# A hybrid decoder layer on one Trainium2 core: the last block's top-k queued behind the gate build, four U chunks held for its end, the late pools split in two, index transposes queued behind U chunks

## The chip, the cores and the metric

The kernel runs on one core of a Trainium2 chip, as one program without loops at run time: the Python loops below are unrolled into one instruction stream for each engine. The engines are PE (matmuls), DVE (VectorE), ACT (ScalarE), POOL (GpSimd) and SP, which only issues DMAs here. The metric is the device time of one execution in microseconds; a comparison takes the median of several.

## The reference, cut to what matters

One decoder layer for 512 tokens of width 1024: a normalised, modulated input goes through latent attention and retention, an output projection and a residual; then comes PEER, a layer of 16384 one-neuron experts, and a last RMSNorm. The change lies in PEER:

```python
q = (xt @ w_query).reshape(T, 8, 2, 128)
s = jnp.einsum('thpd,pkd->thpk', q, sub_keys)          # 8 heads x 2 halves x 128 keys
s_top, i_top = lax.top_k(s, 16)
cand = s_top[:, :, 0, :, None] + s_top[:, :, 1, None, :]
best, pos = lax.top_k(cand.reshape(T, 8, 256), 16)      # 128 experts a token
eidx = ...                                              # i*128 + j of the chosen pairs
g = softmax(best)
a = gelu(einsum('thkd,td->thk', expert_u[eidx], x))
out = einsum('thk,thkd->td', g * a, expert_v[eidx])
```

## The kernel before, in words

The 512 tokens are four blocks of 128. PEER is computed in two ways. Blocks 0 to 2 (`DB`) go the dense way: all 16384 experts are applied to all 384 tokens, with a gate that is zero where an expert was not chosen. Block 3 (`GB`) goes the sparse way: POOL gathers the chosen rows of `expert_u` and `expert_v` by indirect DMA, 128 of each, and DVE multiplies and sums them.

Products in float32 are made of three matmuls (`mm3`) on a rounded part and its remainder: for every streamed weight chunk ACT makes `hi` and DVE or POOL makes `lo` (`split`, L70).

**Top-k** (`topk`, L606). For each block DVE finds the 16 best of 128 for 8 heads and 2 halves, then the 16 best of 50 candidate sums, and turns positions into indices with one-hot comparisons in float16 tiles `t4k`. A softmax follows (one Exp on ACT). For dense blocks the indices and gates are transposed on PE (L673 to L675, under `tc.high_priority()`) into `it` and `gt`. For block 3 they become the index list `eidx` (L667) and `gsm`. The tiles of the pool `topk` are single-buffered, so blocks share them: the index tile `i1` and the tile `iF` that the transposes read are one buffer.

**U chunks** (`u_chunk`, L736). One of 128 chunks of 128 experts: a 512 KB load (`raw`, three buffers), hi and lo, 24 matmuls of 384 columns into a PSUM bank `ab` (two), and a Gelu into `ga` or `gb`. There are 26 `ga` and 11 `gb` buffers: chunk c with c mod 37 below 26 goes into `ga`, others into `gb`; chunk 37 needs chunk 0's.

**Gate build** (`g_steps`, L759). For 8 tokens a step, 48 steps in all: DVE writes four one-hot tiles (L770 to L773, `ohs`, three buffers), PE multiplies them, ACT copies the products into `stg` (two buffers of 2 MB), and after every fourth step SP stores `stg` to DRAM (`Gd`, L786), 12 stores.

**V chunks** (`v_load`, `v_mm`). For 128 experts: `vraw` is loaded, hi and lo made (lo on POOL while U chunks are left), the gate tile `gtl` (L796) is read back from `Gd` once in four chunks, DVE multiplies it with `ga` into `wf` (L807), ACT and DVE split that into `wh` and `wl`, and 18 matmuls add into six PSUM banks.

**Order of the work.** The program is traced in the order of the code. Tile's scheduler then orders each engine's instructions by a simulated time line and by their place in the trace, so an instruction that is traced late can be placed early where its engine would idle. The engines execute in that fixed order and wait at semaphores. Inside `tc.manual_schedule` an engine keeps the traced order. In the code: the top-k of blocks 0 to 2 (L751); 36 U chunks (`R0`) with two gate steps in front of each of the first 24 (L849); the top-k of block 3 (L856); then one pool `late` for everything that follows, which lies where the top-k and gate-build tiles were, with `reuse_waits="tile"`, so that a new tile waits for the old ones under it; then 124 rounds of V chunk c and U chunk c + 36 (L898). Each round adds 2.5 (later 1.12) to a credit, and each whole unit issues one gather step. POOL has manual order from L897, so its vlo and gathers run as traced. The last four V chunks and the final norm close the kernel.

Of the kernel before, what the change touches and what calls it, by code (L numbers as in the profile page):

```python
# [8 lines left out]
F32 = mybir.dt.float32  # L9
# [6 lines left out]
OP = mybir.AluOpType  # L16
# [12 lines left out]
ND = len(DB)  # L29
GB = 3  # L30
# [3 lines left out]
R0 = 36  # L34
RA = 26
NC_ = 50
GPU = 2
GSC = float(2 ** 14)
HB = 2
LB = 4  # L40
CR = (2.5, 1.12)
ORDER = "L m0! p1 d3 p2! m1 p3 d4 p4 d2 p5 p6 r0! r1! p7 r2 r3 X0 X1! d5! m2 g! m3 w0 X3 X2 h0 w1 q0 q1! h1 q2 q3"


# [1 line left out]
def build(ctx: ExitStack, tc: tile.TileContext, A, out):  # L46
    nc = tc.nc
    V, S, P, T, G = nc.vector, nc.scalar, nc.gpsimd, nc.tensor, nc.sync
# [28 lines left out]
    def mm3(o, wh, wl, rh, rl, start, stop, skip=False):  # L77
        T.matmul(o, wh, rh, start=start, stop=False, skip_group_check=skip)  # L78
        T.matmul(o, wh, rl, start=False, stop=False, skip_group_check=skip)  # L79
        T.matmul(o, wl, rh, start=False, stop=stop, skip_group_check=skip)  # L80

    pf = ctx.enter_context(ExitStack())
    ptk = ctx.enter_context(ExitStack())
# [21 lines left out]
    for hf in range(2):  # L105
        p = tpb()
# [49 lines left out]
    hh = cp.tile([128, NB, 8, 128], R, name="hh")  # L156
    hl = cp.tile([128, NB, 8, 128], R, name="hl")
# [445 lines left out]
            w //= 2  # L603
        e.tensor_add(dst, t[:, 0], t[:, 1])

    def topk(b):  # L606
        v1 = tk.tile([128, 8, 2, 16], F32, name="v1", bufs=1)
        i1 = tk.tile([128, 8, 2, 16], U32, name="i1", bufs=1)
        for h in range(8):
# [53 lines left out]
        if b == GB:  # L663
# [2 lines left out]
                                   ij[:, 1].rearrange("p k h -> p (k h)"), op0=OP.mult, op1=OP.add)  # L666
            V.tensor_copy(eidx, ef)  # L667
            return
        with tc.high_priority():
            iF = tk.tile([128, 2, 128], F32, name="i1", bufs=1)  # L670
            V.tensor_copy(iF, ij.rearrange("p q k h -> p q (k h)"))
            p = ob()
            T.transpose(p[:, :128], iF[:, 0], ident)  # L673
            T.transpose(p[:, 128:256], iF[:, 1], ident)
            T.transpose(p[:, 256:384], gg, ident)  # L675
            it = tk.tile([128, 2, 128, 2], F16, name=f"it{b}")
            gt = tk.tile([128, 2, 128, 2], F16, name=f"gt{b}")
            two = lambda a, n: a[:, :, None].to_broadcast([128, n, 2])
            S.activation(it.rearrange("p q t w -> p (q t) w"), two(p[:, :256], 256), AF.Copy)
            S.activation(gt[:, 0], two(p[:, 256:384], 128), AF.Copy, scale=GSC)  # L680
            V.scalar_tensor_tensor(gt[:, 1], two(p[:, 256:384], 128), GSC, gt[:, 0], op0=OP.mult, op1=OP.subtract)
# [51 lines left out]
    NT = ND * 128  # L733
    gas = {}

    def u_chunk(c, lo_engine):  # L736
        raw = raw_t()
        G.dma_start(raw, A["uT"][c])
        hi, lo = split(raw, lo_engine)
        p = ab()  # L740
        for k in range(8):
            ks = slice(k * 128, (k + 1) * 128)
            mm3(p[:, :NT], hi[:, ks], lo[:, ks], hh[:, :ND, k, :], hl[:, :ND, k, :], k == 0, k == 7)
        if c % (R0 + 1) < RA:
            ga = dn.tile([128, NT], F32, name="ga", bufs=RA)
        else:
            ga = dn2.tile([128, NT], F32, name="gb", bufs=R0 + 1 - RA)
        S.activation(ga, p[:, :NT], AF.Gelu)  # L748
        gas[c] = ga

    for b in DB:  # L751
        topk(b)
    pf.close()

    Gd = dram.tile([NIG, ND * 128 // TGS, 128, IGN, TGS], F32, name="Gd")
# [3 lines left out]
    def g_steps():  # L759
        for d, b in enumerate(DB):  # L760
            ij, gg = idxT[b], gT[b]
            for tg in range(128 // TGS):
                stg = gp.tile([128, 128, TGS], F32, name="stg", bufs=2)
                for t8 in range(TGS // 8):
                    t0 = tg * TGS + t8 * 8
                    ohs = gp.tile([128, 4, 8, 128], F16, name="ohs", bufs=3)
                    oh = [ohs[:, q].rearrange("p t (a w) -> p t a w", w=2) for q in range(4)]
                    io = iota_h.rearrange("p (a w) -> p a w", w=2)[:, None].to_broadcast([128, 8, 64, 2])
                    bc = lambda a: a[:, t0:t0 + 8, None, :].to_broadcast([128, 8, 64, 2])
                    V.tensor_tensor(oh[0], io, bc(ij[:, 1]), op=OP.is_equal)  # L770
                    V.tensor_tensor(oh[1], io, bc(ij[:, 0]), op=OP.is_equal)
                    V.tensor_tensor(oh[2], oh[1], bc(gg[:, 0]), op=OP.mult)
                    V.tensor_tensor(oh[3], oh[1], bc(gg[:, 1]), op=OP.mult)  # L773
                    for t4 in range(2):
                        p = tpb() if t4 else acc()
                        for t in range(4):
                            u = t4 * 4 + t
                            cs = slice(t * 128, (t + 1) * 128)
                            T.matmul(p[:, cs], ohs[:, 0, u], ohs[:, 2, u], start=True, stop=False)
                            T.matmul(p[:, cs], ohs[:, 0, u], ohs[:, 3, u], start=False, stop=True)  # L780
                        o0 = t8 * 8 + t4 * 4
                        S.activation(stg[:, :, o0:o0 + 4], p.rearrange("p (t i) -> p i t", t=4), AF.Copy,
                                     scale=1.0 / GSC)
                    yield
                ti = d * (128 // TGS) + tg
                G.dma_start(Gd[:, ti].rearrange("g j i t -> j g (i t)"),  # L786
                            stg.rearrange("p (g i) t -> p g (i t)", i=IGN))
# [32 lines left out]
    gacc = []  # L820

    def gather(table, s):
        r = lp.tile([128, 1024], F32, name="grow", bufs=4)
        P.indirect_dma_start(out=r, out_offset=None, in_=A[table],  # L824
                             in_offset=bass.IndirectOffsetOnAxis(ap=eidx[:, s:s + 1], axis=0))
        return r

    def gather_steps():
        for s in range(128):
            r = gather("expert_u", s)  # L830
            jk = st.tile([128, 1024], BF, name="junk", bufs=1)
            V.scalar_tensor_tensor(jk, r, 1.0, h2n, op0=OP.mult, op1=OP.mult, accum_out=asl[:, s:s + 1])  # L832
            yield
        S.activation(wsl, asl, AF.Gelu)
        V.tensor_mul(wsl, wsl, gsm)
        for i in range(2):
            g = lp.tile([128, 1024], F32, name=f"gacc{i}")
            gacc.append(g)
        for s in range(128):
            r = gather("expert_v", s)  # L840
            g = gacc[s % 2]
            if s < 2:
                V.tensor_scalar(g, r, wsl[:, s:s + 1], None, op0=OP.mult)
            else:
                V.scalar_tensor_tensor(g, r, wsl[:, s:s + 1], g, op0=OP.mult, op1=OP.add)  # L845
            yield

    gs = g_steps()
    for c in range(R0):  # L849
        for _ in range(GPU):  # L850
            next(gs, None)
        u_chunk(c, P if c < 8 else V)
    for _ in gs:
        pass
    pg_.close()
    topk(GB)  # L856
    ptk.close()
    lp = ctx.enter_context(tc.tile_pool(name="late", bufs=1, side="right", reuse_waits="tile"))
    gt2 = lp.tile([128, 1024], F32, name="gt2")
    row_bc(5, gt2)  # L860
    h2n = lp.tile([128, 1024], F32, name="h2n")
    G.dma_start(h2n, h2d)
    gfb = lp.tile([128, 1024], F32, name="gfb")
    G.dma_start(gfb, A["g_final"].partition_broadcast(128))
    asl = lp.tile([128, 128], F32, name="asl")
    wsl = lp.tile([128, 128], F32, name="wsl")
    vacc += [acc() for _ in range(3)] + [tpb() for _ in range(2)] + [ob()]
    ga_it = gather_steps()

    h01 = (slice(0, 512), slice(512, 1024))  # L870

    def final_x(b):
        x2 = raw_t()
        G.dma_start(x2, x2d[b])
        t = lp.tile([128, 1024], F32, name="grow", bufs=4)
        ss = lp.tile([128, 2], F32, name="ssf", bufs=2)
        return x2, t, ss

    def final_h(f, hf, p, eng):
# [5 lines left out]

    def final_b(b, f):
        x2, t, ss = f
        rr = lp.tile([128, 1], F32, name="rrf", bufs=2)
        V.tensor_add(rr, ss[:, 0:1], ss[:, 1:2])
        V.tensor_scalar(rr, rr, 1.0 / D, EPS, op0=OP.mult, op1=OP.add)  # L890
        P.tensor_tensor(rr, rr, mhalf[:, :1], op=OP.pow)
        for cs in h01:
            V.scalar_tensor_tensor(t[:, cs], x2[:, cs], rr, gfb[:, cs], op0=OP.mult, op1=OP.mult)
            G.dma_start(out[b * 128:(b + 1) * 128, cs], t[:, cs])

    credit = 0.0
    ctx.enter_context(tc.manual_schedule(engines={mybir.EngineType.Pool}))  # L897
    for c in range(NK - LB):  # L898
        w = v_load(c)
        for d in range(ND):  # L900
            v_mm(c, w, d)
        if c + R0 < NK:
            u_chunk(c + R0, V)
        credit += CR[0] if c + R0 < NK else CR[1]
        while credit >= 1:
            credit -= 1
            next(ga_it, None)
# [87 lines left out]
```

## Time and profile before

| | us |
|---|---|
| median of 3 runs (1637.5 to 1643.1) | 1642.41 |
| the profiled execution | 1639.2 |
| its span | 1637.3 |
| busy PE / DVE / POOL / ACT | 1522.5 / 1303.1 / 893.8 / 622.7 |

The span runs from the first to the last instruction. The engines' busy shares of the whole span (93%, 80%, 55%, 38%) mix stages with different limits, so the stages are read apart: the front of the layer up to about 440 us, top-k and gate build with U chunks up to about 690, the loop of U and V chunks up to about 1470, V chunks alone and the final norm to the end. "PEclk" is the granted TensorE clock in parts of full speed.

### The profile page before, as it was taken

The page shows a single profiled execution, that of the slowest core. Times are in us where ns is not written, and L with a number is a line of the kernel's source. Part 1 is how long each engine was busy: PE and PEld are TensorE (multiplying, and loading weights), DVE is VectorE, ACT ScalarE, POOL GpSimd, SP SyncE. Part 2 cuts the span into 40 slices and gives each one's busy share as a digit, 9 for nine tenths or more (in the row PEclk, how much of TensorE's full clock was granted, in tenths as well). Part 3 has the DMA queues.
Part 4 walks back from the last instruction along what each step waited for, and adds up shares of the span by engine and source line. Part 5 has one row for each costly group of instructions (what it writes and reads, how often), then busy time and mean ns, then how long its engine had stood idle before and what let it go on. Part 6 is the DMA issues. An engine that isn't in the chain of part 4 may idle for free.

```text
span 1637.3 us, 24259 instructions
## 1 busy us (share of the span) xinstructions
PE 1522.5 (93%) x8977; PEld 1375.7 (84%) x8977; DVE 1303.1 (80%) x2315; ACT 622.7 (38%) x1009; POOL 893.8 (55%) x521
## 2 busy tenths in 40 slices
PE   6899999997878999769999999999999999999977
PEld 6889987797878998667999999999999999988866
DVE  7975754639999999959888787788877887798874
ACT  4433244444424554433333333333333333333322
POOL 4532742775530000058777777777676767775544
PEclk9999999999999999779999999999999999999999
DMA  9455440554325667699989888889988898989853
GB/s 359 156 197 168 143 144 29 183 162 142 104 77 175 211 204 223 208 302 321 337 306 315 286 317 312 296 304 310 333 310 295 301 334 295 321 304 308 284 186 103
DMA packets 196041, 395.63 MB, mean 242 GB/s; under 512 B 12241, under 2 KB 111569, under 8 KB 195922
## 3 DMA queue, kind: packets, MB, share of 16 engines
q1 hardware_dynamic: 157906, 257.22, 46.4%
q0 software_dynamic: 36864, 134.23, 23.5%
q10 hardware_dynamic: 1152, 2.62, 0.4%
q8 instruction: 70, 1.15, 0.3%
q14 instruction: 49, 0.40, 0.1%
HBM read 364.15 MB, written 29.88 MB: 241 GB/s over the span
## 4 chain that ended last, share of the span: by engine, by line
PE 65%; DVE 21%; DMA 5%; issue 4%; POOL 4%; ACT 1%; SPq 0%; DVEq 0%; POOLq 0%; ACTq 0%
PE ab L80 8%; PE ab L78 8%; PE ab L79 8%; PE acc L80 7%; PE acc L78 7%; PE acc L79 7%; PE tp L78 3%; PE tp L79 3%; PE tp L80 3%; DVE lo L74 2%; PE ob L80 1%; PE ob L79 1%; PE ob L78 1%; DVE gacc L845 1%; DVE ohs L770 1%
## 5 line engine op out<-in xcount | busy, mean ns | idle before, releaser
L74 POOL TENSOR_TENSOR vlo<-vraw,vhi 128x1024 fp32r<-128x1024 f32 x92 | 235.7, 2561 | 345.7 <-ACT vhi L73 345.1
L78 PE MATMUL ab<-hh,hi 128*128 128x384 f32 x1024 | 347.1, 339 | 21.7 <-ACT ga L748 19.5
L73 ACT ACTIVATE hi<-raw 128x1024 fp32r<-128x1024 f32 x204 | 216.1, 1060 | 391.4 <-PE ab L79 264.7
L80 PE MATMUL ab<-hh,lo 128*128 128x384 f32 x1024 | 347.7, 340 | 3.8 <-DVE lo L74 2.7
L79 PE MATMUL ab<-hl,hi 128*128 128x384 f32 x1024 | 346.3, 338 | 0.0
L74 POOL TENSOR_TENSOR lo<-raw,hi 128x1024 fp32r<-128x1024 f32 x71 | 181.3, 2556 | 178.6 <-ACT hi L73 170.7
L832 DVE SCALAR_TENSOR_TENSOR junk<-grow,h2n 128x1024 bf16<-128x1024 f32 x128 | 208.6, 1629 | 65.3 <-DMA grow<-in_expert_u_dram,eidx 64.2
L845 DVE SCALAR_TENSOR_TENSOR gacc<-grow,wsl,gacc 128x1024 f32<-128x1024 f32 x126 | 206.4, 1649 | 57.8 <-DMA grow<-in_expert_v_dram,eidx 55.9
L78 PEld LDWEIGHTS ab<-hh,hi 128*128 128x128 f32 x1024 | 193.7, 189 | 26.8 <-ACT ga L748 20.6
L824 POOL DMA_INDIRECT grow<-in_expert_u_dram,eidx x128 | 183.2, 1431 | 39.9 <-issue 22.7
L80 PEld LDWEIGHTS ab<-hh,lo 128*128 128x128 f32 x1024 | 193.6, 189 | 5.7 <-DVE lo L74 4.1
L79 PEld LDWEIGHTS ab<-hl,hi 128*128 128x128 f32 x1024 | 193.7, 189 | 3.4
L824 POOL DMA_INDIRECT grow<-in_expert_v_dram,eidx x128 | 173.5, 1355 | 37.8 <-issue 23.0
L74 DVE TENSOR_TENSOR lo<-raw,hi 128x1024 fp32r<-128x1024 f32 x133 | 171.7, 1291 | 22.9 <-ACT hi L73 16.6
L809 ACT ACTIVATE wh<-wf 128x384 fp32r<-128x384 f32 x110 | 57.8, 525 | 276.4 <-issue 229.2
L79 PE MATMUL acc<-vlo,wh 128*128 128x512 f32 x330 | 129.3, 392 | 9.5 <-DVE vlo L74 5.8
L73 ACT ACTIVATE vhi<-vraw 128x1024 fp32r<-128x1024 f32 x110 | 115.2, 1049 | 39.2 <-DMA vraw<-in_expert_v_dram 39.2
L80 PE MATMUL acc<-vhi,wl 128*128 128x512 f32 x330 | 130.0, 394 | 0.0
L78 PE MATMUL acc<-vhi,wh 128*128 128x512 f32 x330 | 128.8, 397 | 0.0
L78 PE MATMUL acc<-hi,hh 128*128 128x256 f32 (+2 forms) x296 | 91.6, 317 | 6.3 <-ACT hi L73 3.8
L810 DVE TENSOR_TENSOR wl<-wf,wh 128x384 fp32r<-128x384 f32 x110 | 85.5, 777 | 14.6 <-ACT wh L809 14.5
L79 PE MATMUL acc<-lo,hh 128*128 128x256 f32 (+2 forms) x296 | 93.4, 316 | 1.5 <-DVE lo L74 0.8
(339 smaller groups left out, 3332.2 us busy)
## 6 DMA issues: line engine op xcount, KB each, us to landing
raw<-in_uT_dram SPq DMA_DIRECT2D x128, 512.0 KB
vraw<-in_expert_v_dram SPq DMA_DIRECT2D x110, 512.0 KB
Gd<-stg SPq DMA_DIRECT2D x12, 2048.0 KB
gtl<-Gd SPq DMA_DIRECT2D x32, 768.0 KB
raw<-in_wadaT_dram SPq DMA_DIRECT2D x40, 512.0 KB
raw<-in_w_query_dram SPq DMA_DIRECT2D x32, 512.0 KB
raw<-in_expert_v_dram SPq DMA_DIRECT2D x18, 512.0 KB
raw<-in_w_out_dram SPq DMA_DIRECT2D x16, 512.0 KB
```

Of the source, the lines that this page charges most:

```text
L73: S.activation(hi[:, :n], raw[:, :n], AF.Copy)
L74: lo_engine.tensor_sub(lo[:, :n], raw[:, :n], hi[:, :n].bitcast(F32))
L78: T.matmul(o, wh, rh, start=start, stop=False, skip_group_check=skip)
L79: T.matmul(o, wh, rl, start=False, stop=False, skip_group_check=skip)
L80: T.matmul(o, wl, rh, start=False, stop=stop, skip_group_check=skip)
L770: V.tensor_tensor(oh[0], io, bc(ij[:, 1]), op=OP.is_equal)
L809: S.activation(wh, wf, AF.Copy)
L810: V.tensor_sub(wl, wf, wh.bitcast(F32))
L824: P.indirect_dma_start(out=r, out_offset=None, in_=A[table], in_offset=bass.IndirectOffsetOnAxis(ap=eidx[:, s:s + 1], axis=0))
L832: V.scalar_tensor_tensor(jk, r, 1.0, h2n, op0=OP.mult, op1=OP.mult, accum_out=asl[:, s:s + 1])
L845: V.scalar_tensor_tensor(g, r, wsl[:, s:s + 1], g, op0=OP.mult, op1=OP.add)
```

## The change

The second number in `UF` is the count of U chunks that are traced ahead of the top-k of that block. `tc.issue_after(ins)` places each instruction that its block traces on ins's engine behind `ins` in that engine's order; it adds no semaphore. So the index transposes of blocks 1 and 2 stand behind U chunk 7 and 15 on PE, the held chunks' matmuls behind the last gate matmul and their lo behind the last one-hot, and all DVE instructions of block 3's top-k behind the last one-hot. The gate build gets three steps a chunk over chunks 16 to 31, one step being left for the end. Block 3's top-k is traced after two rounds of the V loop. The pool `late` becomes `vside` (V tiles, opened after the gate build) and `gside` (gather and final tiles, opened after block 3's top-k); manual order of POOL begins there.

```diff
+HOLD = 4
+UF = {1: 8, 2: 16}
+LEAD = 2
-CR = (2.5, 1.12)
+CR = (2.56, 1.12)
...
-        with tc.high_priority():
+        with tc.issue_after(after) if after else tc.high_priority():
             iF = tk.tile([128, 2, 128], F32, name="i1", bufs=1)
...
+    def u_load(c):
+        raw = raw_t()
+        G.dma_start(raw, A["uT"][c])
+        return raw
+    def u_chunk(c, lo_engine, raw=None):
+        raw = u_load(c) if raw is None else raw
...
+        last["u"] = m.ins
...
+    nu = 0
     for b in DB:
-        topk(b)
+        while nu < UF.get(b, 0):
+            u_chunk(nu, P if nu < 8 else V)
+            nu += 1
+        topk(b, last.get("u"))
...
     gs = g_steps()
-    for c in range(R0):
-        for _ in range(GPU):
-            next(gs, None)
+    left = ND * 16
+    for c in range(nu, R0 - HOLD):
+        n = -(-left // (R0 - HOLD - c))
+        for _ in range(min(n, left - 1)):
+            next(gs)
+            left -= 1
         u_chunk(c, P if c < 8 else V)
+    held = [u_load(c) for c in range(R0 - HOLD, R0 - HOLD + 3)]
     for _ in gs:
         pass
+    with tc.issue_after(last["g"]):
+        with tc.issue_after(last["o"]):
+            for i, c in enumerate(range(R0 - HOLD, R0)):
+                u_chunk(c, V, held[i] if i < 3 else None)
     pg_.close()
-    topk(GB)
-    ptk.close()
-    lp = ctx.enter_context(tc.tile_pool(name="late", bufs=1, side="right", reuse_waits="tile"))
+    lp = ctx.enter_context(tc.tile_pool(name="vside", bufs=1, reuse_waits="tile"))
...
     for c in range(NK - LB):
+        if c == LEAD:
+            with tc.issue_after(last["o"]):
+                topk(GB)
+            ptk.close()
+            lg = ctx.enter_context(tc.tile_pool(name="gside", bufs=1, side="right", reuse_waits="tile"))
+            h2n = lg.tile([128, 1024], F32, name="h2n")
+            G.dma_start(h2n, h2d)
...
+            ga_it = gather_steps(h2n, asl, wsl)
+            ctx.enter_context(tc.manual_schedule(engines={mybir.EngineType.Pool}))
         w = v_load(c)
         for d in range(ND):
             v_mm(c, w, d)
         if c + R0 < NK:
             u_chunk(c + R0, V)
+        if c < LEAD:
+            continue
         credit += CR[0] if c + R0 < NK else CR[1]
```

`last["o"]` is the last one-hot (L773), `last["g"]` the last gate matmul (L780).

## Rows read from the trace of the kernel before

**Rows 1.** Busy time by stretch: length, engines with (xinstructions), PE clock, DMA share, GB/s
```profile
464.30:694.30 230.00, 208.86 (x1642) 196.44 (x1641) 226.75 (x661) 107.36 (x177) 7.21 (x3) 0.95 0.60 187
...
800.00:1400.00 600.00, 600.00 (x3048) 546.90 (x3047) 485.07 (x497) 212.79 (x291) 438.48 (x254) 1.00 0.88 310
...
688.00:700.00 12.00, 3.26 (x22) 2.52 (x20) 5.91 (x14) 2.28 (x4) 0.00 (x0) 0.50 0.66 193
700.00:712.00 12.00, 3.25 (x10) 3.25 (x11) 3.26 (x6) 4.98 (x7) 1.49 (x1) 0.50 0.92 299
...
609.00:610.00 1.00, 1.00 (x7) 1.00 (x6) 1.00 (x9) 0.00 (x0) 0.00 (x0) 1.00 0.95 291
```

**Rows 2.** Waits of PE and DVE, 400 to 720 us: total, times, longest
```profile
PE ab L78 <- ACT ga L748: 19.5, 3, 16.8
PE ob L673 <- DVE i L671: 18.2, 2, 9.7
...
DVE wf L807 <- DMA gtl<-Gd: 11.5, 1, 11.5
```

**Rows 3.** Single lines: count, duration, first and last start (L748, L74, L786)
```profile
L748 ACT ACTIVATE ga<-ab x32: 466/472/512, 447.0 to 763.5; 128x384 f32<-128x384 f32 x32
L748 ACT ACTIVATE gb<-ab x11: 471/472/493, 606.3 to 664.5; 128x384 f32<-128x384 f32 x11
...
L74 DVE TENSOR_TENSOR lo<-raw,hi x33: 1200/1221/1240, 492.5 to 679.0; 128x1024 fp32r<-128x1024 f32 x33
...
L786 SPq DMA_DIRECT2D Gd<-stg x12: 377/377/383, 503.9 to 690.8; - x12
```

**Rows 4.** DVE in order of time: start, duration, instruction, [idle before, releaser]
```profile
393.81 3.23 DVE L643 TENSOR_TENSOR t4k<-t4k,dd 128x2048 f16<-128x2048 f16 x1
...
463.21 0.29 DVE L671 CAST i<-ij 128x256 f32<-128x256 f16 x1
...
659.36 0.70 DVE L771 TENSOR_TENSOR ohs<-iota_h,it 128x1024 f16<-128x1024 f16 x1
659.96 0.70 DVE L772 TENSOR_TENSOR ohs<-ohs,gt 128x1024 f16<-128x1024 f16 x1
...
661.89 1.23 DVE L74 TENSOR_TENSOR lo<-raw,hi 128x1024 fp32r<-128x1024 f32 x1
663.01 0.71 DVE L770 TENSOR_TENSOR ohs<-iota_h,it 128x1024 f16<-128x1024 f16 x1
...
675.43 1.23 DVE L643 TENSOR_TENSOR t4k<-t4k,dd 128x2048 f16<-128x2048 f16 x1
...
687.28 0.70 DVE L773 TENSOR_TENSOR ohs<-ohs,gt 128x1024 f16<-128x1024 f16 x1
...
694.02 0.23 DVE L667 CAST eidx<-bpos 128x128 int32<-128x128 f32 x1
705.78 1.03 DVE L807 TENSOR_TENSOR wf<-ga,gtl 128x384 f32<-128x384 f32 x2 [11.53 <-DMA gtl<-Gd]
```

**Rows 5.** The chain that ended last, 685 to 705 us: start, length
```profile
690.81 9.34 DMA Gd<-stg
```

**Rows 6.** ACT in order of time, two Gelus in the loop
```profile
763.45 0.47 ACT L748 ACTIVATE ga<-ab 128x384 f32<-128x384 f32 x1
...
771.74 0.47 ACT L748 ACTIVATE ga<-ab 128x384 f32<-128x384 f32 x1
```

**Rows 7.** POOL in order of time, front and start of the V loop
```profile
393.37 2.58 POOL L74 TENSOR_TENSOR lo<-raw,hi 128x1024 fp32r<-128x1024 f32 x1 [1.70 <-ACT hi L73]
...
710.51 2.37 POOL L74 TENSOR_TENSOR vlo<-vraw,vhi 128x1024 fp32r<-128x1024 f32 x1 [229.20 <-ACT vhi L73]
...
715.53 2.41 POOL L74 TENSOR_TENSOR vlo<-vraw,vhi 128x1024 fp32r<-128x1024 f32 x1
```

**Rows 8.** PE in order of time, U chunk 39 behind the hole
```profile
709.56 0.52 PE L80 MATMUL ab<-hh,lo 128*128 128x384 f32 x1
709.88 0.52 PE L78 MATMUL ab<-hh,hi 128*128 128x384 f32 x1
```

More of the change, by code (lines that the diff above doesn't have):

```diff
@@ L79, in mm3 @@
         T.matmul(o, wh, rl, start=False, stop=False, skip_group_check=skip)
-        T.matmul(o, wl, rh, start=False, stop=stop, skip_group_check=skip)
+        return T.matmul(o, wl, rh, start=False, stop=stop, skip_group_check=skip)
     pf = ctx.enter_context(ExitStack())
@@ L604, in tree, with topk @@
         e.tensor_add(dst, t[:, 0], t[:, 1])
-    def topk(b):
+    def topk(b, after=None):
         v1 = tk.tile([128, 8, 2, 16], F32, name="v1", bufs=1)
@@ L734, in build @@
     gas = {}
-    def u_chunk(c, lo_engine):
+    last = {}
+    def u_load(c):
         raw = raw_t()
         G.dma_start(raw, A["uT"][c])
+        return raw
+    def u_chunk(c, lo_engine, raw=None):
+        raw = u_load(c) if raw is None else raw
         hi, lo = split(raw, lo_engine)
@@ L742, in u_chunk @@
             ks = slice(k * 128, (k + 1) * 128)
-            mm3(p[:, :NT], hi[:, ks], lo[:, ks], hh[:, :ND, k, :], hl[:, :ND, k, :], k == 0, k == 7)
+            m = mm3(p[:, :NT], hi[:, ks], lo[:, ks], hh[:, :ND, k, :], hl[:, :ND, k, :], k == 0, k == 7)
+        last["u"] = m.ins
         if c % (R0 + 1) < RA:
@@ L772, in g_steps @@
                     V.tensor_tensor(oh[2], oh[1], bc(gg[:, 0]), op=OP.mult)
-                    V.tensor_tensor(oh[3], oh[1], bc(gg[:, 1]), op=OP.mult)
+                    last["o"] = V.tensor_tensor(oh[3], oh[1], bc(gg[:, 1]), op=OP.mult).ins
                     for t4 in range(2):
@@ L779, in g_steps @@
                             T.matmul(p[:, cs], ohs[:, 0, u], ohs[:, 2, u], start=True, stop=False)
-                            T.matmul(p[:, cs], ohs[:, 0, u], ohs[:, 3, u], start=False, stop=True)
+                            m = T.matmul(p[:, cs], ohs[:, 0, u], ohs[:, 3, u], start=False, stop=True)
+                            last["g"] = m.ins
                         o0 = t8 * 8 + t4 * 4
@@ L822, in gather @@
     def gather(table, s):
-        r = lp.tile([128, 1024], F32, name="grow", bufs=4)
+        r = lg.tile([128, 1024], F32, name="grow", bufs=4)
         P.indirect_dma_start(out=r, out_offset=None, in_=A[table],
@@ L826, in gather, with gather_steps @@
         return r
-    def gather_steps():
+    def gather_steps(h2n, asl, wsl):
         for s in range(128):
@@ L836, in gather_steps @@
         for i in range(2):
-            g = lp.tile([128, 1024], F32, name=f"gacc{i}")
+            g = lg.tile([128, 1024], F32, name=f"gacc{i}")
             gacc.append(g)
@@ L848, in build @@
     gs = g_steps()
-    for c in range(R0):
-        for _ in range(GPU):
-            next(gs, None)
+    left = ND * 16
[4 more added lines that the diff above has]
+            left -= 1
         u_chunk(c, P if c < 8 else V)
+    held = [u_load(c) for c in range(R0 - HOLD, R0 - HOLD + 3)]
     for _ in gs:
         pass
+    with tc.issue_after(last["g"]):
+        with tc.issue_after(last["o"]):
+            for i, c in enumerate(range(R0 - HOLD, R0)):
+                u_chunk(c, V, held[i] if i < 3 else None)
     pg_.close()
-    topk(GB)
-    ptk.close()
-    lp = ctx.enter_context(tc.tile_pool(name="late", bufs=1, side="right", reuse_waits="tile"))
+    lp = ctx.enter_context(tc.tile_pool(name="vside", bufs=1, reuse_waits="tile"))
     gt2 = lp.tile([128, 1024], F32, name="gt2")
     row_bc(5, gt2)
[L861 to L866, printed above, removed]
     vacc += [acc() for _ in range(3)] + [tpb() for _ in range(2)] + [ob()]
-    ga_it = gather_steps()
+    ga_it, lg = None, None
     h01 = (slice(0, 512), slice(512, 1024))
@@ L874, in final_x @@
         G.dma_start(x2, x2d[b])
-        t = lp.tile([128, 1024], F32, name="grow", bufs=4)
-        ss = lp.tile([128, 2], F32, name="ssf", bufs=2)
+        t = lg.tile([128, 1024], F32, name="grow", bufs=4)
+        ss = lg.tile([128, 2], F32, name="ssf", bufs=2)
         return x2, t, ss
@@ L887, in final_b @@
         x2, t, ss = f
-        rr = lp.tile([128, 1], F32, name="rrf", bufs=2)
+        rr = lg.tile([128, 1], F32, name="rrf", bufs=2)
         V.tensor_add(rr, ss[:, 0:1], ss[:, 1:2])
@@ L896, in build @@
     credit = 0.0
-    ctx.enter_context(tc.manual_schedule(engines={mybir.EngineType.Pool}))
     for c in range(NK - LB):
+        if c == LEAD:
[5 more added lines that the diff above has]
+            G.dma_start(h2n, h2d)
+            gfb = lg.tile([128, 1024], F32, name="gfb")
+            G.dma_start(gfb, A["g_final"].partition_broadcast(128))
+            asl = lg.tile([128, 128], F32, name="asl")
+            wsl = lg.tile([128, 128], F32, name="wsl")
+            ga_it = gather_steps(h2n, asl, wsl)
+            ctx.enter_context(tc.manual_schedule(engines={mybir.EngineType.Pool}))
         w = v_load(c)
```

## The prediction

> **What bounds the kernel now.** I read the busy times by stretch first. They give three regimes. From 800 to 1400 us PE is busy 600.00 of 600 us at clock 1.00, with DVE at 485 and POOL at 438: the U/V loop is bound by PE, and whatever reaches it earlier ends earlier. From 464.3 to 694.3 us DVE is busy 226.75 of 230 us, so the gate build and the top-k are bound by DVE (PE 208.86, POOL 7.21). From 688 to 712 us neither works: PE 6.5 of 24 us, DVE 9.2, granted clock 0.50 [rows 1]. The waits say who ended that hole: the longest PE wait, 16.8 us, is for a Gelu, and the DVE wait of 11.5 us is for gtl [rows 2]. The Gelu is that of U chunk 37: the last gb, chunk 36, was written at 664.5 [rows 3], and that was the last free buffer; the next slot comes with the first wf, which needs gtl, which needs the last gate store. So the chain through the hole is last one-hot (687.28), store (issued 690.81, landed 9.34 later, at 700.15), then gtl, wf at 705.78 [rows 4, 5]. The last block's top-k ended inside it, with eidx at 694.02 [rows 4].
>
> Two pitches carry the sum. In the loop one U and one V chunk take 771.74 - 763.45 = 8.29 us, 4.145 a chunk [rows 6]. On DVE a one-hot starts every 0.60 us (659.36, 659.96), so a gate step of four costs 2.40; a lo costs 663.01 - 661.89 = 1.12 [rows 4].
>
> **What one top-k costs DVE.** From the end of the second block's index cast (463.5) to that of eidx (694.25) lie 230.75 us [rows 4]. Take off 48 gate steps x 2.40 = 115.2, 33 lo [rows 3] x 1.12 = 37.0, and 3.3 idle (230 - 226.75): 75.3 us remain for two top-ks, 37.6 each.
>
> **The change, part by part.**
>
> *Last top-k behind the gate build.* On DVE it removes 37.6 us from ahead of the last one-hot and puts it behind. The U chunks done by then are 0 to 31, so DVE has 24 lo before the end instead of 33. New last one-hot: 463.5 + 37.6 (third block) + 115.2 + 24 x 1.12 (26.9) + 3.3 idle + 2 (index transposes, below) = 648.5, against 688. PE must allow it: of its 208.86 us, 36 chunks (U3 to U38) are 149.2, so the gate build is 59.7, some 56 without the slow clock of its end. After: 29 chunks (120.2) + 56 = 176 us between 455 (463.5 without the wait of 8.5 for the second block's indices, below) and 648.5, 91% as now.
>
> *Four held U chunks.* Their loads go out before the last gate step, and their matmuls and lo stand behind it. Chunks 36 and later cannot pass them, since they take the same three raw buffers. They give PE 16.6 us, to about 667 counting 2 us for the last gate matmuls. The store lands near 648.5 + 3.5 (the distance of 690.81 from 687.28) + 9.34 = 661.5, gtl 5.6 later at 667 (705.78 - 700.15) [rows 4, 5]: the hole is covered. Without that cover it costs its 16.8 us again.
>
> *Pools split, LEAD = 2.* By itself it costs no instruction. V tiles no longer need the top-k's space, so V0, U36, V1, U37 follow the held chunks: another 16.6 us, to 683.
>
> *What is late next: eidx.* Behind the last one-hot DVE has 37.6 of top-k, 6 lo (U32 to U37, 6.7) and wf and wl of two chunks at half of the 1.03 row each (about 2.1). To this come two costs that no row shows in this place. (1) POOL is idle beside today's last top-k and will be running vlo beside the new one. A 2048-element f16 product took 3.23 us when it met a POOL subtraction (393.81 beside 393.37) and 1.23 alone at 675.43 [rows 4, 7]. None to three of the vlo before eidx can meet such an op: 0 to 7 us; I take two meetings, 4. (2) wf(0) stands in DVE's order where the planner believes gtl lands; what is behind it, the top-k, waits with it. 0 if it is placed late, 11.5 if it is placed first [rows 2]; I take 4, near the idle that planned stretch has now. eidx: 648.5 + 37.6 + 6.7 + 2.1 + 4 + 4 = 703. The Exp and its table loads move along on ACT, which has room.
>
> The Trainium skill bears on (1). Its page "SBUF — State Buffer", section "Who interferes with whom", says that a VectorE instruction with two SBUF inputs and a GpSimd one that reads SBUF exclude each other, the second blocked until the first is done. The trace agrees: 3.23 is about 2.0 over 1.23, most of the 2.58 us subtraction. By the rule all three vlo would block, about 3 us more than I take; it is the rule that speaks against this move.
>
> *POOL's queue.* vlo(3) stands behind the first two gathers, and they wait for eidx. From one vlo to the next with two gathers between took 715.53 - 710.51 = 5.02 [rows 7], so vlo(3) ends 5 us after eidx, 708, and V3 can start at 709. PE has V2 and U38 until 691 and then waits, unless U39 and later were planned ahead. After such a wait PE restarts at half rate: matmuls 0.32 apart (709.56, 709.88) [rows 8], about half of the loop's rate, over one chunk; 1.8 us.
>
> *h2n and g_final loads (512 KB each).* They leave SP's queue between the last store and gtl and go behind U37's load, waiting for the top-k's space; the loads of V3 and U39 queue behind them. At 291 GB/s, the rate of a store at 609 us [rows 1], they are 1.8 us each, inside the wait for V3: 0, at most 3.6 if that wait is gone.
>
> *Index transposes behind U7 and U15.* PE's two waits for them are 18.2 us together; the first block keeps its 9.7, the second's 8.5 goes [rows 2]. Worth 0, since DVE is the bound; it pays for PE's share above. New wait: the third block's index tile shares a buffer with the second's, read by transposes that now follow U7, at 455 + 5 x 4.145 = 476 instead of 463.5. DVE's FIND_INDEX can be held 0 to 12.5 us; lo and maxima are there to fill it, so I take 2. U15 ends near 509, before the third top-k: nothing.
>
> *Three gate steps a chunk, CR 2.56.* Same instructions. 90 x 2.56 + 32 x 1.12 = 266 gather steps against 92 x 2.5 + 32 x 1.12 = 266: the gathers end in the same chunk. An extra 0.06 row an iteration lies under a full PE [rows 1].
>
> **Sum.** Before, Gelu 42 at 763.45 says that PE was through U42 and V6. After, from V3 at 709: V3 to V6 and U39 to U42, 8 x 4.145 = 33.2, and 1 us to the Gelu: 743.2. That is 20.2 earlier, less 1.8 for the slow restart: 18.4. The rest of the loop and the tail move along. The profiled run took 1639.2 us (span 1637.3): 1620.8. The median of the runs lies 3.2 above it; I add half, 1622.
>
> **Rivals.**
> - *PE never waits.* The planner sees that V3 is late and pulls U39 to U43 ahead, which wf's two buffers allow. For: it ran U37 and U38 ahead before the hole. Against: it trusts its own estimate of the top-k, and twice put transposes 9 us too early [rows 2]. The wait of about 18 us and the restart are saved: 1603.
> - *Nothing gained.* The doubtful waits come at their upper ends: wf(0) first (7.5 more) and FIND_INDEX held (10.5 more) put eidx at 721, and the top-k becomes what starts the loop, as the store does now: 1640.
> - *Slower: the stores set the gate build.* Today a store leaves every (690.8 - 503.9) / 11 = 17.0 us [rows 3]. In my sum it is (648.5 - 510) / 12 = 11.5 (510 is 463.5 with the third top-k and eight lo behind it), with two stg buffers, so a store must land within about one such interval. 2 MB at 291 GB/s are 7.2 us, with the DMA engines at 0.95 [rows 1], and U loads (1.8 each) share the queue. Landing of 9.34 plus two loads in front, 3.6, plus 1.2 for the evictions is 14.1: 12 x 2.6 = 31 later, 1653. It decides from 11.5 + 18.4 / 12 = 13.0 us a store. Against: only 1.3 loads come to a store.
>
> **How the numbers follow.** Forecast 0.47 (its own range 1611 to 1633), never waits 0.20, nothing gained 0.19, slower 0.14. Below 1602 I leave 0.08 and above 1647 0.10. This kernel's measurement can tell 0.5%, 8.2 us, from no change: faster takes nearly all of the first case, the second, and a little of the third, 0.68; the same 0.18; slower 0.14.
>
> **What would show it.** Right: no PE hole behind the last gate matmul, last one-hot near 648, eidx near 703, then a PE wait on POOL's vlo of 10 to 20 us with a clock dip, Gelu 42 near 743, PE full from there. Wrong: stores 13 us or more apart with ACT waiting on stg; DVE waiting for gtl ahead of the top-k; or PE fed straight through, and then the gain is nearer 37.

## The result, and the profile after

The changed kernel takes 1616.89 us (median of 4 runs, 1614.58 to 1620.02) against 1641.87 for the kernel before on the same chip: ratio 0.9841, 95% interval 0.9814 to 0.9869, 25 us faster. The forecast was 1622, within 1602 to 1647. The profiled execution took 1614.58 (span 1612.4, 24.9 less than before).

The stretches after, with the columns of [rows 1]; the first runs from where the third block's top-k has started to the end of the gate build, the last is the loop:

```profile
466.00:655.00 189.00, 170.10 (x1401) 159.74 (x1400) 179.12 (x429) 93.24 (x156) 2.41 (x1) 0.93 0.63 194
606.00:655.00 49.00, 33.10 (x344) 29.48 (x342) 49.00 (x82) 24.70 (x44) 0.00 (x0) 0.72 0.72 216
655.00:770.00 115.00, 108.00 (x551) 98.11 (x550) 106.72 (x299) 42.61 (x59) 52.08 (x29) 0.99 0.78 260
770.00:1370.00 600.00, 597.86 (x3032) 543.98 (x3031) 511.89 (x524) 213.59 (x291) 468.42 (x266) 1.00 0.91 320
```

The three regimes are still there, but the hole of 688 to 712 is gone: from 655 to 770 PE works 108.00 of 115 us. The weak stretch is now 606 to 655, where DVE has nothing but one-hots (49.00 of 49), PE 33.10, at a mean granted clock of 0.72: U0 to U31 were done by 606.73, and the gate steps left over ran alone.

The waits after, 400 to 740 us (total, times, longest), against [rows 2]:

```profile
ACT stg L797 <- PE acc L794: 30.6, 19, 4.1
...
POOL grow L839 <- DVE eidx L670: 26.9, 1, 26.9
...
PE acc L793 <- DVE ohs L786: 12.2, 11, 3.3
...
PE ob L676 <- DVE i L674: 9.6, 1, 9.6
DVE lo L77 <- ACT hi L76: 8.9, 4, 4.7
...
DVE i L597 <- PE ob L677: 3.0, 2, 2.2
...
PE ab L81 <- ACT ga L758: 0.6, 1, 0.6
```

PE's 19.5 us on a Gelu has become 0.6, and DVE's wait for gtl has no row any more. One of PE's two waits for the index cast is left. New are DVE's wait of 8.9 for hi and POOL's of 26.9 for eidx; DVE's wait for the transposes grew from 1.6 to 3.0.

DVE in order of time around the top-k, against [rows 4]: last one-hot 653.21 (before 687.28), eidx 715.08 (before 694.02).

```profile
653.21 0.72 DVE L787 TENSOR_TENSOR ohs<-ohs,gt 128x1024 f16<-128x1024 f16 x1
...
677.35 2.16 DVE L825 TENSOR_TENSOR wl<-wf,wh 128x384 fp32r<-128x384 f32 x1 [0.50 <-ACT wh L824]
...
679.89 2.29 DVE L825 TENSOR_TENSOR wl<-wf,wh 128x384 fp32r<-128x384 f32 x1
...
686.44 2.32 DVE L631 TENSOR_TENSOR cd<-v 128x64 f32<-128x64 f32 x1
688.68 0.55 DVE L825 TENSOR_TENSOR wl<-wf,wh 128x384 fp32r<-128x384 f32 x1
...
715.08 0.23 DVE L670 CAST eidx<-bpos 128x128 int32<-128x128 f32 x1
```

POOL, against [rows 7]; vlo(3) stands behind two gathers, as forecast:

```profile
675.76 6.01 POOL L77 TENSOR_TENSOR vlo<-vraw,vhi 128x1024 fp32r<-128x1024 f32 x2 [206.04 <-DVE v L596]
686.28 2.40 POOL L77 TENSOR_TENSOR vlo<-vraw,vhi 128x1024 fp32r<-128x1024 f32 x1 [4.51 <-ACT vhi L76]
715.61 1.90 POOL L839 DMA_INDIRECT grow<-in_expert_u_dram,eidx  x1 [26.93 <-DVE eidx L670]
717.81 0.94 POOL L839 DMA_INDIRECT grow<-in_expert_u_dram,eidx  x1 [0.30 <-issue]
718.78 2.41 POOL L77 TENSOR_TENSOR vlo<-vraw,vhi 128x1024 fp32r<-128x1024 f32 x1
```

The store that once ended the hole, on the chain that ended last after (start, length), against [rows 5], and all 12 stores, against [rows 3]: (657.0 - 521.8) / 11 = 12.3 us apart.

```profile
657.00 10.94 DMA Gd<-stg
668.06 0.38 SPq L811
```

```profile
L801 SPq DMA_DIRECT2D Gd<-stg x12: 360/377/428, 521.8 to 657.0; - x12
```

How far ahead the loop is can be read from any Gelu in it. The 81st, U80, first before, then after:

```profile
1078.10 0.47 ACT L748 ACTIVATE ga<-ab 128x384 f32<-128x384 f32 x1
```

```profile
1059.39 0.47 ACT L758 ACTIVATE ga<-ab 128x384 f32<-128x384 f32 x1
```

The loop is 18.7 us ahead here; U100 gives 19.2, U120 19.8. (1.3 us of this lie ahead of the change: the first block's index cast starts at 412.18 before and at 410.86 after.) The last 5 us to 24.9 come behind the loop.

### The profile page after: what moved, and what is told of

Its sections match the earlier page's. It is cut to its first block, busy times and chain, and to the rows that moved or that the text cites. A ratio compares the mean times of both kernels' runs of the same rounds, so it can differ in the third digit from the quotient of the medians.

```text
span 1612.4 us, 24255 instructions
## 1 busy us (share of the span) xinstructions
PE 1520.5 (94%) x8977; PEld 1375.7 (85%) x8977; DVE 1318.9 (82%) x2315; ACT 625.3 (39%) x1009; POOL 910.3 (56%) x521
## 4 chain that ended last, share of the span: by engine, by line
PE 57%; DVE 18%; DMA 12%; issue 7%; POOL 4%; ACT 1%; SPq 0%; DVEq 0%; POOLq 0%; ACTq 0%
PE ab L83 8%; PE ab L81 8%; PE ab L82 8%; PE acc L82 6%; PE acc L83 6%; PE acc L81 6%; DMA grow<-in_expert_u_dram,eidx 3%; DMA raw<-in_wadaT_dram 2%; PE tp L82 2%; PE tp L83 2%; PE tp L81 2%; DVE gacc L860 2%; DMA gtl<-Gd 1%; DVE junk L133 1%; DMA vraw<-in_expert_v_dram 1%
## 5 line engine op out<-in xcount | busy, mean ns | idle before, releaser
L77 POOL TENSOR_TENSOR lo<-raw,hi 128x1024 fp32r<-128x1024 f32 x71 | 185.9, 2621 | 156.6 <-ACT hi L76 148.7
L847 DVE SCALAR_TENSOR_TENSOR junk<-grow,h2n 128x1024 bf16<-128x1024 f32 x128 | 213.7, 1670 | 42.9 <-DMA grow<-in_expert_u_dram,eidx 41.3
L860 DVE SCALAR_TENSOR_TENSOR gacc<-grow,wsl,gacc 128x1024 f32<-128x1024 f32 x126 | 196.0, 1566 | 57.3 <-DMA grow<-in_expert_v_dram,eidx 57.0
L839 POOL DMA_INDIRECT grow<-in_expert_v_dram,eidx x128 | 181.5, 1418 | 42.4 <-issue 19.3
L77 DVE TENSOR_TENSOR lo<-raw,hi 128x1024 fp32r<-128x1024 f32 x133 | 183.6, 1381 | 24.8 <-ACT hi L76 24.8
L81 PE MATMUL acc<-vhi,wh 128*128 128x512 f32 x330 | 122.1, 390 | 0.1
L825 DVE TENSOR_TENSOR wl<-wf,wh 128x384 fp32r<-128x384 f32 x110 | 91.7, 834 | 13.6 <-ACT wh L824 13.5
```

Of the source, the lines that this page charges most:

```text
L77: lo_engine.tensor_sub(lo[:, :n], raw[:, :n], hi[:, :n].bitcast(F32))
L825: V.tensor_sub(wl, wf, wh.bitcast(F32))
L839: P.indirect_dma_start(out=r, out_offset=None, in_=A[table], in_offset=bass.IndirectOffsetOnAxis(ap=eidx[:, s:s + 1], axis=0))
```

## The experiments

The account of the prediction is that the moved top-k carries the gain; the rivals are named in each expectation. Ratios are to the kernel before, on the same chip. "One-hot" is the start of the last one-hot, "eidx" that of its cast. The part up to 440 us is the same code in all kernels, yet it shifts by up to 8 us between profiled executions: the first block's index cast starts between 406.94 (only the top-k's move) and 415.13 (no held chunks). Late times carry that much scatter. The last four runs are from another chip, where the kernel before takes 1644.63 us, so they are compared with the others by their ratios.

**No held chunks.** All else as in the changed kernel.

```diff
-HOLD = 4
+HOLD = 0
-    held = [u_load(c) for c in range(R0 - HOLD, R0 - HOLD + 3)]
+    held = []
```

> The changed kernel with no U chunk held: all 36 are traced among the gate steps. Theory 1 (the end of DVE's last top-k, eidx at 715 us, sets where the loop starts): PE has some 30 free us between 608 and 655 and takes U32 to U35 there, eidx stays near 715 and V3 near 722; the time stays within 4 us of the changed kernel's 1617. Rival (the held chunks are what fills the hole behind the last gate store): PE has only U36 to U38 between 655 and the first V at 677, stands 10 us or more, and the time is 1627 or more.

1614.36 us, 0.9830 (0.9799 to 0.9861); one-hot 668.79, eidx 721.32. The hole is back (PE's wait, then the stretches):

```profile
PE acc L81 <- ACT wh L824: 15.7, 1, 15.7
```

```profile
606.00:655.00 49.00, 47.83 (x452) 44.29 (x450) 46.54 (x71) 27.88 (x48) 0.00 (x0) 1.00 0.80 249
655.00:770.00 115.00, 88.42 (x490) 78.45 (x490) 108.98 (x311) 38.94 (x58) 46.79 (x27) 0.88 0.75 249
```

From 655 us on PE loses 19.6 us (88.42 for 108.00), and from 606 to 655 it works 14.7 more (47.83 for 33.10, and at clock 1.00 for 0.72). Counted from the first block's index cast, the last one-hot comes 11.3 us later than in the changed kernel and eidx 2.0, yet the time is the same. Holding chunks moves PE's idle time from behind the gate build into it, and is worth nothing here.

**Top-k in its old place,** held chunks and the other edits kept.

```diff
     pg_.close()
+    topk(GB)
...
-            with tc.issue_after(last["o"]):
-                topk(GB)
```

> The changed kernel with the last block's top-k traced in front of the V loop and not tied behind the last one-hot, so that the planner may place it among the gate steps as before. Theory 1 (DVE order): the last one-hot moves from 654 to about 690 and the first gtl from 668 to about 704; the held chunks cover part of it; V3 starts no earlier than 730; the time is 1625 to 1640. Rival (held chunks are the gain): hole covered all the same, 1615 to 1622.

1642.61 us, 1.0005 (0.9985 to 1.0024); one-hot 689.84, eidx 696.07. The whole gain goes, with the chunks held. Its waits, 400 to 740 us, the first of PE, the second of DVE:

```profile
PE acc L793 <- DVE ohs L786: 30.3, 21, 3.6
```

```profile
DVE wf L822 <- DMA gtl<-Gd: 6.3, 1, 6.3
```

PE no longer waits 16.8 us at once, but 30.3 in 21 pieces in the gate build, and Gelu U80 starts at 1084.02, 5.9 us behind the kernel before. Without the top-k's new place the other parts gain nothing together.

**Index transposes back in front.** No U chunk ahead of a top-k, so no `issue_after` on the transposes.

```diff
-UF = {1: 8, 2: 16}
+UF = {}
```

> The changed kernel with no U chunks ahead of the top-k of blocks 1 and 2, index transposes at high priority again. Theory 1: PE's wait for the second block's indices comes back (8 to 9 us at 455) but DVE's work up to eidx is the same; within 4 us of 1617, and if anything faster, since DVE's own waits for hi (8.9 us) and for the transposes (3.0 us) came with those chunks. Rival (the waits of PE are the gain): 8.5 us slower, 1625.

1603.92 us, 0.9773 (0.9734 to 0.9812), 13 us faster than the changed kernel by the medians, 11 by the ratios, where 4 at most were expected; one-hot 645.88, eidx 706.54. PE's second wait for the indices is back (18.2 us for both), and DVE's waits shrink (lo on hi 8.9 to 2.6). The stretch in which the transposes move, after first, then this kernel:

```profile
460.00:484.00 24.00, 23.54 (x136) 22.86 (x134) 16.93 (x69) 8.87 (x13) 7.18 (x3) 1.00 0.35 110
```

```profile
460.00:484.00 24.00, 22.32 (x120) 22.32 (x121) 23.08 (x136) 6.63 (x10) 7.22 (x3) 0.89 0.21 67
```

In the changed kernel PE gains 1.2 us here and DVE, the bound of this regime, loses 6.2.

**U8 to U15's lo on POOL,** with the rest as changed: does the lo that DVE waits with set the price?

```diff
-            u_chunk(nu, P if nu < 8 else V)
+            u_chunk(nu, P)
```

> The changed kernel with lo of U8 to U15 on POOL instead of DVE; POOL is idle there. Theory 1 (DVE's work up to eidx is the bound): DVE loses eight lo (9 us) and its waits for hi (8.9 us), the last one-hot comes at 636 to 646 instead of 654 and eidx at 700 to 706; the time is 1603 to 1611. Rival (a POOL subtraction blocks DVE's two-input operations for 2 us each): 16 us come back, 1617 to 1624.

1615.56 us, 0.9841 (0.9812 to 0.9871): no change; one-hot 655.23, eidx 717.0. The wait for hi fell from 8.9 to 5.1 us and that for the transposes grew from 3.0 to 8.9; from 460 to 484 us DVE works 15.72 of 24. The expectation missed. Eight lo are 9 us of DVE's work. From the first block's index cast to the last one-hot DVE idles 2.9 us more than in the changed kernel, and three of its instructions beside POOL's lo grow by 4.7 us in all (a one-hot takes 2.32 for 0.68): the rival, POOL in DVE's way, has a share too.

**Only the top-k's move, with the split pools.**

```diff
-HOLD = 4
-UF = {1: 8, 2: 16}
+HOLD = 0
+UF = {}
...
-        n = -(-left // (R0 - HOLD - c))
+        n = GPU
```

> Only the last block's top-k behind the gate build, with the two pools that this needs: no U chunks ahead of the other top-ks, no held chunks, two gate steps a chunk as before. Theory 1 (the top-k's place in DVE's order is the whole gain, the chunks in front of the other top-ks cost 8 to 13 us): as without those chunks, 1604, within 5 us. Rival (holding chunks matters once DVE's waits are gone): 1612 or more.

1609.17 us, 0.9814 (0.9782 to 0.9845); one-hot 649.16, eidx 705.83. The interval overlaps that of the run with UF empty and the chunks held: the move, with the split pools and the new credit, gives all of the gain. What the pools and the credit give without the move was not run alone.

**The lo of U0 to U31 on POOL,** which stands idle there. UF empty as well.

```diff
-        u_chunk(c, P if c < 8 else V)
+        u_chunk(c, P)
```

> No U chunks ahead of the top-ks, and lo of all U chunks up to 31 on POOL, which idles there: DVE is freed of 24 lo of 1.12 us, 27 us. Theory P (a POOL subtraction and a DVE operation with two SBUF inputs exclude each other; 2.0 us a meeting in the trace before): 24 x 2.0 = 48 us come back, one-hots start 21 us later in sum, eidx moves from 707 to 720 to 730, time 1615 to 1630. Rival (DVE simply loses the work): eidx near 680, time 1580 to 1590.

1635.66 us, 0.9963 (0.9941 to 0.9985): 32 us slower than without this edit; one-hot 669.71. Between 480 and 655 us, a kind of one-hot on DVE with UF empty alone, then the same line and POOL's lo here (last numbers: busy, mean ns, idle before):

```profile
L785 DVE TENSOR_TENSOR ohs<-iota_h,it 128x1024 f16<-128x1024 f16 x48 | 32.9, 684 | 0.0
```

```profile
L785 DVE TENSOR_TENSOR ohs<-iota_h,it 128x1024 f16<-128x1024 f16 x43 | 38.0, 884 | 0.0
...
L77 POOL TENSOR_TENSOR lo<-raw,hi 128x1024 fp32r<-128x1024 f32 x22 | 83.8, 3814 | 90.7 <-ACT hi L76 87.2 <-PE tp L794 3.4
```

POOL idle beside a busy DVE is not a free engine here: 22 lo taken from DVE save 22 x 1.22 = 26.8 us, but the one-hots lengthen from 0.68 to between 0.81 and 0.88 us (means of the four kinds), 29.9 us over the 171 in this stretch, and each lo takes 3.8 us on average in place of the 2.40 of one alone. So DVE's saving is used up. The engines then also wait for each other: from 400 to 740 us PE stands 11.4 us for a lo of POOL (0.9 without this edit) and DVE 15.8 for PE (3.8). PE falls from 165.92 to 146.69 of 175 us. The expectation, 1615 to 1630, had the mechanism and too small a size.

**Gathers later,** UF empty, first gathers in round 5 in place of 2.

```diff
-CR = (2.56, 1.12)
+CR = (2.65, 1.12)
...
-        if c < LEAD:
+        if c < 5:
```

> No U chunks ahead of the top-ks, and the first gathers are issued after V chunk 5 instead of V chunk 2 (credit 2.65 for 2.56), so that POOL's subtractions for V3 to V5 do not stand behind eidx. My forecast's step (eidx, two gathers, vlo(3) set the start of the V loop): V3 could start near 695 instead of 713, and 5 us or more are gained, 1594 to 1599. Rival (PE has U38 to U41 to run and does not wait for V3): within 4 us of 1604.

1600.03 us, 0.9760 (0.9727 to 0.9793); one-hot 645.08, eidx 712.38. vlo(3) now runs at 681.34, without waiting for eidx. The median is 4 us under that with UF empty alone, and the intervals overlap: at most a small gain. There was little to win: with UF empty alone PE waits 1.6 us in all for vlo.

**Top-k traced at once behind the gate build.** UF empty.

```diff
-LEAD = 2
+LEAD = 0
```

> No U chunks ahead of the top-ks, and the last top-k traced in front of V0 instead of behind two rounds. If the planner follows the trace, V0, U36, V1 and U37 stand behind the top-k on DVE, eidx comes some 6 us earlier and PE idles up to 16 us behind U35: 1608 to 1616. Rival (the planner fills by readiness, the place in the trace matters little): within 4 us of 1604.

1613.25 us, 0.9826 (0.9796 to 0.9857), 9 us slower than with LEAD = 2; eidx 709.42, 58.8 us behind the one-hot (60.7 with LEAD = 2). PE waits 6.5 and 2.9 us for Gelu buffers again, and the second vlo comes only at 712.42. Traced first, the top-k ends only 2 us sooner after the gate build, and the V chunks pay for it.

**Only the top-k's move, with the gathers from round 5.**

```diff
-HOLD = 4
-UF = {1: 8, 2: 16}
+HOLD = 0
+UF = {}
...
-CR = (2.56, 1.12)
+CR = (2.65, 1.12)
...
-        n = -(-left // (R0 - HOLD - c))
+        n = GPU
...
-        if c < LEAD:
+        if c < 5:
```

> Only the last block's top-k behind the gate build and its two pools, as in the run with that alone, and the first gathers after V chunk 5 (credit 2.65). If the two gains are independent (no chunks ahead of the other top-ks; vlo(3) not behind eidx), it is the fastest so far: 1594 to 1602. If they are the same waiting taken away twice, it stays at 1604 to 1610.

1602.53 us (6 runs), 0.9766 (0.9730 to 0.9802). The interval overlaps those of UF empty alone and of the later gathers before: nothing is told apart.

**Top-k and gathers later still,** from the run before.

```diff
-LEAD = 2
+LEAD = 5
-CR = (2.65, 1.12)
+CR = (2.75, 1.12)
-        if c < 5:
+        if c < 8:
```

> As the last one, with the top-k traced in front of V chunk 5 instead of 2 and the first gathers after V chunk 8 (credit 2.75). Theory 1 (DVE has slack in the loop, 115 of 600 us before, and the top-k fits into it without holding up the first V chunks): eidx later by 8 to 15 us, PE fed from the store on, 3 to 8 us faster than the last one. Rival (the loop then needs 2.75 rows an iteration and DMA, at 0.91 and 320 GB/s with 2.56, becomes its bound): 1605 or more, PE below 590 of 600 in the loop.

1603.49 us, 0.9759 (0.9726 to 0.9793). The same again, and neither side of the expectation came: eidx stays at 717.53 (717.07 in the run before), and the loop is full, with the DMA engines at 0.91:

```profile
770.00:1370.00 600.00, 599.99 (x3054) 547.83 (x3053) 515.06 (x534) 212.70 (x292) 465.16 (x272) 1.00 0.91 325
```

**U chunks first, but transposes as before.** UF as changed; the transposes keep their priority.

```diff
-        topk(b, last.get("u"))
+        topk(b)
```

> The changed kernel with 8 and 16 U chunks still traced ahead of the second and third top-k, but the index transposes at high priority instead of behind U7 and U15 on PE. If the transposes' place costs (FIND_INDEX held): DVE's wait for them (2.2 us) goes, 1612 to 1616. If the chunks' place costs (DVE stands at lo of U8 and later, waiting for hi, 8.9 us): DVE's waits for hi stay, 1613 to 1620. The time decides little; DVE's waits in the trace tell them apart.

1609.68 us, 0.9804 (0.9760 to 0.9848); one-hot 647.9, eidx 708.54, 6.5 us earlier than in the changed kernel. DVE waits, 400 to 740 us:

```profile
DVE lo L77 <- ACT hi L76: 2.8, 3, 1.7
...
DVE i L597 <- PE ob L677: 1.6, 2, 0.8
```

Both waits that the expectation set against each other shrink. Gelu U80 starts at 1048.10, 11.3 us earlier than in the changed kernel, about as with UF empty (1049.54). By the trace the price of this part hangs on the edge behind U7 and U15, not on the chunks' place; the time alone does not tell this run from the changed kernel, since the intervals overlap.

**The kernel before, with that part alone.**

```diff
+    nu = 0
     for b in DB:
-        topk(b)
+        while nu < {1: 8, 2: 16}.get(b, 0):
+            u_chunk(nu, P if nu < 8 else V)
+            nu += 1
+        topk(b, last.get("u"))
```

> The kernel before with one part of the change alone: 8 and 16 U chunks ahead of the second and third top-k, their index transposes behind those chunks, three gate steps a chunk. My forecast put this part at nothing (0 to 12.5 us lost). By the runs so far it costs DVE some 8 us: last one-hot and eidx later by 5 to 10 us than 687 and 694, 1645 to 1652. Rival (PE's 8.5 us wait for the indices goes and that is a gain here): 1632 to 1637.

1651.81 us, 1.0059 (1.0030 to 1.0088): slower by itself, and the time as expected. One-hot 702.91, eidx 708.64: some 15 us later than before, where 5 to 10 were expected. Waits of PE and DVE, 400 to 740 us: the hole is as it was, and DVE's wait for hi is there.

```profile
PE ab L80 <- ACT ga L751: 20.5, 4, 17.0
```

```profile
DVE lo L74 <- ACT hi L73: 4.9, 2, 4.7
```

## Why the prediction was right, and where not

**The total: right.** Sum 18.4 us for the loop; measured 18.7 at U80, 19.8 at U120. That the top-k's place carries it is shown from both sides: back in its place the gain is gone (1.0005); with nothing but the split pools and the credit beside it, it is all there (0.9814).

**Last one-hot: 648.5, measured end 653.9.** The DVE count was sound; the 5 us are about the idle time that the transposes put into DVE (below). With UF empty the last one-hot starts at 645.88.

**eidx: 703, measured 715.** Five of the 12 us come from there. The rest lies between the last one-hot and eidx, 61.4 us where I had 54.5: DVE ran 10 lo and 7 wf there, for my 6 lo and the wf and wl of two chunks, since the planner had pulled later chunks ahead. Lines of that stretch (653.8 to 715.4), columns as above:

```profile
L77 DVE TENSOR_TENSOR lo<-raw,hi 128x1024 fp32r<-128x1024 f32 x11 | 13.6, 1245 | 0.0
L825 DVE TENSOR_TENSOR wl<-wf,wh 128x384 fp32r<-128x384 f32 x5 | 6.1, 1224 | 0.5 <-ACT wh L824 0.5
...
L822 DVE TENSOR_TENSOR wf<-ga,gtl 128x384 f32<-128x384 f32 x7 | 3.8, 575 | 0.0
```

(The eleventh lo starts behind eidx.) Four lo more are 4.5 us; wf and wl are 3.8 + 6.1, less the 2.1 I had and the 3.4 of contention (next), 4.4 more; contention is 1.4 over my 4; and the 4 for a wait on gtl did not come, DVE waiting 0.5 in all. That makes 6.8 of the 6.9.

**POOL's vlo beside DVE: 4, measured about 5.4.** wl takes 2.16 and 2.29 beside the pair of vlo at 675.76 and 0.55 alone (3.4 more); cd takes 2.32 beside the vlo at 686.28, about 2 more than its like. All three vlo ahead of eidx met such an instruction, where I had taken two. The Trainium skill's page "SBUF — State Buffer", section "Who interferes with whom", says that a VectorE instruction with two SBUF inputs and a GpSimd one that reads SBUF exclude each other. The trace agrees in the count of meetings; its price, 5.4, lies between the 4 taken and the 7 that stood as the upper end. The run with lo on POOL shows that over a long stretch both engines pay.

**PE behind V2: wrong, in mechanism and not in sum.** I had V3 wait for vlo(3) with PE idle from 691 to 709. vlo(3) did come late, and later than I said (718.78), but PE ran U38 to U41 meanwhile, the rival's mechanism: its waits for vlo are 1.6 us in all, not 10 to 20, and Gelu 42 came at 729.39, not near 743.

```profile
729.39 0.47 ACT L758 ACTIVATE ga<-ab 128x384 f32<-128x384 f32 x1
```

So at U42 PE was 34.1 us ahead on the U side (763.45 before), and at vlo(6), 743.44 against 750.53, 7.1 us on the V side. If a U and a V chunk cost the same, as the forecast took them, the mean of the two, 20.6, is a rough count of PE's lead, close to the loop's 18.7. My 12 us too early for eidx and 18 us of idle PE that did not come nearly cancel: this part of the sum was right by compensation. The rival's 1603 did not come, because its mechanism took hold of a later eidx; with UF empty, where eidx comes at 706.54, the time is 1603.92.

**Held chunks: cover for 16.8 us, worth nothing.** The hole left, as forecast (gtl issued 668.06; said 661.5, and U32 to U35 ran 655 to 678). But I did not price what they were taken from: U0 to U31 were done by 606.73, so PE lacked work in the rest of the gate build, and the run without held chunks is as fast, hole and all. A long wait of PE thus showed where its shortage of work lay and not what it cost. For the kernel before, with the top-k in its old place, this is not shown: the run with the top-k there and chunks held (1.0005) is 9 us faster by the ratios than the kernel before with U chunks ahead of the top-ks alone (1.0059), and held chunks, pools and credit all differ between the two.

**Index transposes: 2 (0 to 12.5), measured 6 to 11.** They ran at 474.41 (said 476), so the step was right and its cover wrong. I had named lo and maxima as the work that would fill DVE. But DVE runs its instructions in their fixed order, and there a lo that waits for hi stood first and then the find (the search for the maxima's positions) that waits for the transposes; nothing behind them ran meanwhile:

```profile
471.42 1.23 DVE L77 TENSOR_TENSOR lo<-raw,hi 128x1024 fp32r<-128x1024 f32 x1 [4.75 <-ACT hi L76]
...
474.83 0.09 DVE L597 MATCH_VALUE_LOAD i<-v,blk 128x8 f32 x1 [2.18 <-PE ob L677]
```

DVE loses 6.2 us between 460 and 484. By the ratios the time falls by 11 us with UF empty and by 6 with the edge alone removed (there the intervals overlap), and rises by about 10 when this part is added to the kernel before. The rival "nothing gained" had this mechanism at its upper end (10.5 more); it came in part, and its other half, wf(0) in front of the top-k (I took 4), not at all.

**Stores: the slower rival was wrong.** They left every 12.3 us on average, above the 11.5 of the sum and under the 13.0 that would decide, and what ACT waits for at stg is PE's acc (30.6 us in 19 waits), not the DMA.

**Behind the loop: 0, measured 5.** From Gelu U120 to the end of the span it takes 228.0 us before and 222.9 after. The last gather issues 24.6 us earlier (1537.99 for 1562.57), and PE's waits for lo parts there are shorter; the two kinds before, then after, 1400 to 1640 us:

```profile
PE acc L79 <- DVE vlo L74: 5.8, 4, 2.2
PE acc L79 <- POOL lo L74: 3.7, 2, 2.1
```

```profile
PE acc L82 <- DVE vlo L77: 2.1, 1, 2.1
```

The top-k's place is not the cause. With the top-k in its old place and the new pools and credit the same part takes 225 us, and all other runs with these pools and a larger credit take 219 to 226; the kernel before with U chunks ahead of the top-ks alone, which has the old pools and credit, takes 228.3. Whether the pools or the credit do it was not tried alone and stays open.

**A better version.** The fastest median is UF empty with the gathers from round 5, 1600.03 us, 17 us under the changed kernel by the medians and 13 by the ratios; UF empty alone, 1603.92, is not told apart from it, and neither are the two runs with the top-k's move and later gathers. All of them beat the kernel before and the changed one.

## What to carry to other kernels

In a regime where one engine is the bound, ask of each edit how much of that engine's work lies ahead of the next regime's start, and move out what the next regime can run beside its own bound: here 37.6 us of DVE moved behind the gate build, and the time fell by 25 us. The longest wait of an engine that is not the bound says where its shortage shows, and not yet what it costs; filling it from work that would have run earlier moves the gap. An ordering edge that saves the other engine a wait can stall the bound one in its own in-order queue, so price it there, by what stands behind the stalled instruction and not by what could be run in its place.

## What the runs showed of the hardware

- Lo on POOL beside one-hots on DVE slowed both: one-hots from 0.685 us to 0.81 to 0.88, lo from 2.40 to a mean of 3.81, and the kernel with the lo of U8 to U31 on POOL was 32 us slower than with them on DVE.
- A stretch of gate matmuls alone has PE busy 33.10 of 49 us at a mean granted clock of 0.72 (0.99 from 606 to 613 us, 0.50 from 634 to 641: the levels of 2.4 and 1.2 GHz); with U chunks between them PE is busy 47.83 of the same 49 us at 1.00.
- DMA was no bound in the loop at 325 GB/s and a share of 0.91 (the run with top-k and gathers later still): PE worked 599.99 of 600 us.
